# A gate product between up and down, both halves of down with seven-product units, and token sums from transposed rows

## The chip, the cores and the metric

The kernel runs on one core of a Trainium2 chip. The metric is the device time of one execution in microseconds (us), less is better; the time before is the median of three runs. The core has five engines that work side by side: TensorE (PE) for matmuls, VectorE (DVE), ScalarE (ACT), GpSimd (POOL), and SyncE (SP), which here only starts transfers from main memory (HBM). PE writes its results to eight banks of an accumulator memory (PSUM, 128 x 512 float32 each); everything else lies in the on-chip buffer (SBUF).

## The reference

One decoder layer on 256 tokens with 2048 channels in float32: a feed-forward network (FFN1), a mixing sub-layer with two kinds of attention, and a second network of the same shape (FFN2), each followed by a LayerNorm.

```python
def swiglu(x, w_gate, w_up, w_down):
    return (jax.nn.silu(x @ w_gate) * (x @ w_up)) @ w_down

x = layer_norm(DEEPNORM_ALPHA * x + FFN_RES_WEIGHT * swiglu(x, ffn1_w_gate[l], ffn1_w_up[l], ffn1_w_down[l]),
               ln1_g[l], ln1_b[l])
...
mix = jnp.concatenate([o_mla, o_nsa], axis=-1) @ w_out[l]
x = layer_norm(DEEPNORM_ALPHA * x + mix, ln2_g[l], ln2_b[l])
x = layer_norm(DEEPNORM_ALPHA * x + FFN_RES_WEIGHT * swiglu(x, ffn2_w_gate[l], ffn2_w_up[l], ffn2_w_down[l]),
               ln3_g[l], ln3_b[l])
```

The inner width of the networks is 5632. The change is in the two networks; the attention in between only gets its small tiles from a buffer pool that is cut in another way.

## The kernel before

**Products in three matmuls.** Every float32 operand is split into a rounded high part and a remainder (`split`, lines 80 to 82: ACT casts, DVE subtracts). `mm3` (lines 84 to 88) adds three matmuls for one product of a 128-row tile: high x high (line 86), high x low of the weight (87), low x high (88). So every weight that comes from HBM (`raw`) is cast by ACT into `whi` and gets its remainder `wlo` from DVE before PE can use it. There are five `raw`, three `sum`, six `whi` and six `wlo` buffers of 128 x 1024.

**The networks.** The 5632 inner columns are 11 blocks of 512, numbered 0 to 10, in groups 0 to 3, 4 to 7 and 8 to 10. For each group `ffn` (line 361) makes gate and up two blocks at a time, multiplies them, transposes the product (`hs`, rows are tokens) block by block into `hT`, and then adds the group's share of down to the result `y`. Block 10 of gate and up is made as one pair (`_gu`). The stages in order are: gate 0, 1; up 0, 1; gate 2, 3; up 2, 3; down of the first group (first half of the 2048 output columns, then the second); the same for the second group; gate 8, 9; up 8, 9; the combined product; down of the third group.

**Seven-product units.** `gemm2` (line 218) makes two column blocks for both token tiles at once. It walks over pairs of 128-row k tiles, of which there are eight in a product of gate and up or in the first two groups of down. A plain pair takes eight products, 24 matmuls. A pair listed in `seven` takes seven products (a two-by-two scheme of the Strassen kind), 21 matmuls: DVE first forms sums of the four weight tiles (lines 250 to 252), and the other side needs sums of the four tiles of the moving operand (`sums`, lines 298 to 305, with the pieces `m` made by `parts`). Behind the last such pair four partial results are merged (line 270 on ACT, lines 271 to 274 on DVE), and at the end four more additions join them with the plain part (line 282). Gate has three such pairs (`GATE7`), up four (`UP7`), the combined product four, and down four in the second half of the first two groups (`DOWN7`); the first half of down is plain (`gemm`, line 173).

**Order.** PE and SP run in the order in which the code is written. A clock of ticks (`tick`, `steps`) lets small tasks, such as the transposes, step in between pairs; `held` stops them while all eight PSUM banks are taken. ACT, DVE and POOL get their order from a scheduler, and each then works strictly in it.

**Where the sums of down come from.** When up of a block is multiplied (line 413), `up` starts two kinds of tasks. `go` (line 382) transposes four 128 x 128 tiles of a product on PE and splits them from PSUM. `go2` (line 392) does so for each pair that is to be done with seven products: DVE has formed the four sums from rows of `hs` before, PE transposes the four sums, and ACT and DVE split them from PSUM.

**Other names.** `wk` gives one of nine work tiles `w` of 128 x 512; `am` one of sixteen tiles `m` of the same size for pieces and for small operands of the attention. In FFN2 the list `late` holds four calls of `ln_res` (lines 523 to 531), each with two transfers on POOL's queue (lines 526, 527) and four DVE operations on `y` (530, 531); two calls stand behind each of the first two up products (lines 440 to 442).

## Time and profile before

| | us |
|---|---|
| median of three runs | 1785.65 |
| lowest, highest | 1784.14, 1786.55 |
| the profiled execution | 1784.83 |
| span in its trace | 1783.1 |

The profile is one execution. Its page gives the busy time of each engine, shares of the span, and groups of instructions by source line. The trace behind it is asked for a timeline (every instruction with its start and length), for windows (busy time of every engine in a stretch), and for waits (who waited for whom, inferred from semaphores). Matmuls overlap in the timeline: each starts before the one ahead has ended, so their spacing is read from their starts. Stages are found by counting matmuls of lines 86 to 88 from the start of each network.

FFN1 takes the first 714 us, with gate 4, 5 at 266.3, up 4, 5 at 307.8, gate 6, 7 at 348.6 and up 6, 7 at 391.4 us; the first half of down of the first group begins at 179.2 us. FFN2 begins at 1061.7 us, and its gate 2, 3 at 1151.6 us.

### The profile page before, as it was taken

Reading aid. Unit: us, or ns where it says so; the run is one execution under the profiler, and the core shown is the slowest. Engines: PE = TensorE matmul, PEld = TensorE weight load, DVE = VectorE, ACT = ScalarE, POOL = GpSimd, SP = SyncE. Lnnn points to the kernel's source line nnn. Section 1 sums busy time; section 2 is a strip of 40 time slices with the busy share of each in tenths; the row PEclk is TensorE's granted clock in tenths of the full one; section 3 lists DMA queues with packets and bytes.
Section 4 is the critical chain, followed back from the end, with each engine's and each line's share of the span. In section 5 each row is a group of like instructions: output and inputs, shape, how many; then the busy total and the mean of one; then the engine's idle time right before and its main releaser. Section 6 shows DMA issues by size and latency. Waiting matters only on the chain. (4 is left out here: it accounts for less than half of the span.)

```text
span 1783.1 us, 22369 instructions
## 1 busy us (share of the span) xinstructions
PE 1761.0 (99%) x8132; PEld 1445.5 (81%) x8132; DVE 1499.9 (84%) x1965; ACT 965.1 (54%) x1261; POOL 17.5 (1%) x40
## 2 busy tenths in 40 slices
PE   8999999999999999999999999999999999999997
PEld 6888888888888888887788777878888888888886
DVE  7899789999699986776567687899799998799976
ACT  6556455565456554654455555555456565456541
POOL 0000000000000000000000000000000000000000
PEclk9999999999999999999999999999999999999999
DMA  9666555557456675546743444657555656556673
GB/s 320 228 205 210 176 198 197 189 192 253 146 194 210 199 249 179 183 168 209 266 173 109 138 155 142 198 194 252 163 203 202 202 200 215 172 194 210 205 246 106
DMA packets 119423, 350.01 MB, mean 196 GB/s; under 512 B 11136, under 2 KB 15504, under 8 KB 119312
## 3 DMA queue, kind: packets, MB, share of 16 engines
q1 hardware_dynamic: 118000, 344.37, 57.1%
q0 software_dynamic: 1312, 4.21, 0.9%
q8 instruction: 64, 1.05, 0.2%
q14 instruction: 47, 0.39, 0.1%
HBM read 346.44 MB, written 2.10 MB: 195 GB/s over the span
## 5 line engine op out<-in xcount | busy, mean ns | idle before, releaser
L86 PE MATMUL bank<-whi,thi 128*128 128x512 f32 (+1 forms) x2038 | 804.0, 394 | 2.2 <-ACT thi L81 1.7
L87 PE MATMUL bank<-wlo,thi 128*128 128x512 f32 (+1 forms) x2038 | 792.3, 389 | 1.9 <-DVE wlo L82 1.9
L88 PE MATMUL bank<-whi,tlo 128*128 128x512 f32 (+1 forms) x2038 | 792.5, 389 | 0.1
L81 ACT CAST whi<-raw 128x1024 fp32r<-128x1024 f32 (+2 forms) x534 | 513.0, 977 | 412.4 <-PE bank L88 316.5
L82 DVE TENSOR_TENSOR wlo<-raw,whi 128x1024 fp32r<-128x1024 f32 (+2 forms) x534 | 594.9, 1130 | 104.4 <-ACT whi L81 104.1
L86 PEld LDWEIGHTS bank<-whi,thi 128*128 128x128 f32 x2038 | 383.0, 188 | 83.8 <-issue 4.5
L88 PEld LDWEIGHTS bank<-whi,tlo 128*128 128x128 f32 x2038 | 382.7, 188 | 81.3 <-DVE tlo L82 1.4
L87 PEld LDWEIGHTS bank<-wlo,thi 128*128 128x128 f32 x2038 | 383.1, 188 | 78.5 <-DVE wlo L82 3.7
L81 ACT CAST whi<-sum 128x1024 fp32r<-128x1024 f32 x262 | 271.7, 1048 | 279.9 <-PE bank L88 162.7
L82 DVE TENSOR_TENSOR wlo<-sum,whi 128x1024 fp32r<-128x1024 f32 x262 | 313.8, 1219 | 75.9 <-ACT whi L81 75.4
L87 PE MATMUL bank<-wlo,m 128*128 128x512 f32 x352 | 137.4, 390 | 0.2 <-DVE wlo L82 0.2
L88 PE MATMUL bank<-whi,m 128*128 128x512 f32 x352 | 137.0, 389 | 0.0
L86 PE MATMUL bank<-whi,m 128*128 128x512 f32 x352 | 137.0, 389 | 0.0
L250 DVE TENSOR_TENSOR sum<-raw 128x1024 f32<-128x1024 f32 x88 | 107.6, 1223 | 28.9 <-DMA raw<-in_ffn_w_gate 16.1
L87 PEld LDWEIGHTS bank<-wlo,m 128*128 128x128 f32 x352 | 66.1, 188 | 15.2 <-DVE wlo L82 1.6
L86 PEld LDWEIGHTS bank<-whi,m 128*128 128x128 f32 x352 | 66.1, 188 | 13.7
L88 PEld LDWEIGHTS bank<-whi,m 128*128 128x128 f32 x352 | 66.1, 188 | 13.7
L282 DVE TENSOR_TENSOR w<-bank,w 128x512 f32<-128x512 f32 x96 | 63.1, 686 | 0.0
L252 DVE TENSOR_TENSOR sum<-sum,raw 128x512 f32<-128x512 f32 x88 | 60.7, 690 | 0.7
L251 DVE TENSOR_TENSOR sum<-sum,raw 128x512 f32<-128x512 f32 x88 | 60.5, 688 | 0.3
L82 DVE TENSOR_TENSOR tlo<-bank,thi 128x512 fp32r<-128x512 f32 (+1 forms) x56 | 36.0, 649 | 4.0 <-ACT thi L81 3.6
L672 ACT ACTIVATE w<-w,mx 128x256 f32<-128x256 f32 (+1 forms) x48 | 21.4, 446 | 31.3 <-DVE mx L668 31.3
(187 smaller groups left out, 871.3 us busy)
## 6 DMA issues: line engine op xcount, KB each, us to landing
raw<-in_ffn_w_up SPq DMA_DIRECT2D x160, 512.0 KB, 4.7
raw<-in_ffn_w_gate SPq DMA_DIRECT2D x148, 512.0 KB, 4.8
raw<-in_ffn_w_down SPq DMA_DIRECT2D x134, 512.0 KB, 4.5
sum<-in_ffn_w_down SPq DMA_DIRECT2D x42, 512.0 KB, 6.4
raw<-in_ffn_gu SPq DMA_DIRECT2D x32, 512.0 KB, 4.8
raw<-in_w_in SPq DMA_DIRECT2D x30, 512.0 KB, 4.5
raw<-in_w_out SPq DMA_DIRECT2D x20, 512.0 KB, 3.2
sum<-in_w_in SPq DMA_DIRECT2D x18, 512.0 KB, 5.7
```

Source lines behind the costliest of these rows:

```text
L81: A.copy(hi, src)
L82: V.tensor_tensor(lo, src, f(hi), op=OP.subtract)
L86: PE.matmul(ps, xh, wh, start=first, stop=False)
L87: PE.matmul(ps, xh, wl, start=False, stop=False)
L88: PE.matmul(ps, xl, wh, start=False, stop=last)
L250: V.tensor_tensor(t13, a_, b_[:, 1:2, :].broadcast_to([P, 2, NCH]), op=OP.add)
L251: V.tensor_tensor(t24[:, 0], t13[:, 0], a_[:, 1], op=OP.add)
L252: V.tensor_tensor(t24[:, 1], t24[:, 0], b_[:, 0], op=OP.add)
L282: V.tensor_tensor(r, B[b], r, op=OP.add)
L672: A.activation(s[:, h, :], s[:, h, :], AF.Exp, bias=mx[:, h:h + 1], accum_out=sm[:, h:h + 1])
```

## The change

The stages of a network are written as one list: gate 0, up 0, gate 2, up 2, gate 4, down of the first group, up 4, gate 6, up 6, gate 8, down of the second group, up 8, the combined product, down of the third group (each number stands for two blocks). So a gate product lies between an up product and the down that reads it, and the transposes of that up product are done in its last pairs.

Both halves of down of the first two groups get four seven-product units; the combined product has three instead of four. The pairs of a product are taken in a given order (`GATE`, `UP`, `LATE`, `DOWN`), of which those in the lists with a 7 are seven-product units.

The sums for down are formed from the transposed rows: for blocks 0, 1 (and 4, 5) `trans` copies the transposed tiles from PSUM into a work tile, and DVE forms the sums of that. `go2` and its transposes are gone.

The tiles `m` are twice as wide, eight in place of sixteen, and are handed out as pairs (`am2`). The four calls in `late` stand in the second gate product of blocks 0, 1, which is plain.

```diff
@@ -34,10 +34,13 @@
 O_CKV, O_KR, O_Q, O_KC, O_KS, O_KW, O_G = 512, 768, 832, 1856, 2368, 2880, 3392
 KT = 2
 HEAD, SPARE = 8, 2
-NM = 16
+NM = 8
 NW = 9
-GATE7, UP7 = (2, 4, 5), (1, 2, 4, 5)
-DOWN7 = (((), (1, 2, 4, 5)), ((), (1, 2, 4, 5)), ((), ()))
+
+GATE, GATE7 = (0, 1, 2, 3, 4, 5, 6, 7), (2, 4, 5)
+UP, UP7 = (0, 1, 3, 2, 4, 6, 5, 7), (1, 2, 4, 5)
+LATE = (0, 3, 1, 6, 2, 4, 5, 7)
+DOWN, DOWN7 = (4, 0, 1, 5, 2, 3, 6, 7), (0, 1, 2, 3)
...
     def am(dt=F32):
-        return att.tile([P, 4, P], dt, name="m", bufs=NM)
+        return att.tile([P, 8, P], dt, name="m", bufs=NM)
+
+    def am2(dt=F32):
+
+        m = am(dt)
+        return m[:, 0:4, :], m[:, 4:8, :]
...
-    def gemm2(x, xs, seven, w, cp, kps, finish, each=None):
+    def gemm2(x, xs, kps, seven, w, cp, finish, each=None):
...
-        s_first, s_last = min(seven), max(seven)
+        s_at = [n for n, i in enumerate(kps) if i in seven]
...
-        for i, ops in todo:
+        for at, (i, ops) in enumerate(todo):
+            if at > s_at[-1]:
+                held[0] = False
...
-            if i == s_last:
+            if at == s_at[-1]:
...
-            held[0] = s_first - 1 <= i <= s_last
+            held[0] = s_at[0] - 1 <= at <= s_at[-1]
             tick(1)
             if each:
-                each(i)
...
     def parts(s):
-        hl = am(F32R), am(F32R)
+        hl = am2(F32R)
         split(*hl, s)
...
-        kall = list(range(KD // KT))
-        for gi, grp in enumerate(groups):
-            hT, hS, hs = {}, {}, {}
-            base = 2 * grp[0]
-            seven = [{base + i for i in DOWN7[gi][j]} for j in range(2)]
-
-            def up(c, t, h):
-
-                hs[c, t] = h
-
-                ready = now[0] + DFF
-
-                def go(c=c, t=t):
+        hT, hS, hs, sg = {}, {}, {}, {}
+
+        def trans(cs, ready, sums_too):
+
+            for c in cs:
+                v = []
+                for t in range(NT):
                     while held[0] or now[0] < ready:
                         yield 1
                     pt = new_bank().rearrange("p (a b) -> p a b", a=4)
                     for j in range(4):
                         PE.transpose(pt[:, j, :], hs[c, t][:, j * P:(j + 1) * P], ident)
                     hT[c, t] = new_T()
-                    split(hT[c, t][0], hT[c, t][1], pt)
+                    src = pt
+                    if sums_too:
+                        src = wk([P, 4, P])
+                        A.copy(src, pt)
+                        v.append(src)
+                    A.copy(hT[c, t][0], pt)
+                    V.tensor_tensor(hT[c, t][1], src, f(hT[c, t][0]), op=OP.subtract)
+                    if t and sums_too:
+                        for i in range(KT):
+                            hS[2 * c + i] = parts(sums([u[:, KT * i + j] for u in v for j in range(KT)]))
                     yield 1
-                def go2(i, s):
-                    while held[0] or now[0] < ready:
-                        yield 1
-                    pt = new_bank().rearrange("p (a b) -> p a b", a=4)
-                    for j in range(4):
-                        PE.transpose(pt[:, j, :], s[:, j, :], ident)
-                    hS[i] = parts(pt)
-                    yield 1
-
-                spawn(go(), "T")
-                if t:
-                    for i in (2 * c, 2 * c + 1):
-                        if i in seven[0] | seven[1]:
-                            spawn(go2(i, sums([hs[c, u][:, (2 * (i % 2) + j) * P:(2 * (i % 2) + j + 1) * P]
-                                               for u in range(NT) for j in range(2)])), "T")
-                steps()
-
-            for c0 in grp[::2]:
-                sg = {}
-
-                def gate(t, j, r):
+        def gate(c0):
+            def fin(t, j, r):
+                A.activation(r, r, AF.Silu)
+                sg[c0 + j, t] = r
+
+            if c0:
+                gemm2(x, xs, GATE, GATE7, name + "_w_gate", c0 // 2, fin)
+                return
+            def rest(i):
+                if i % 2 and late:
+                    late.pop(0)()
+
+            for c in range(2):
+                def first(t, ps, c=c):
+                    sg[c, t] = wk([P, NCH])
+                    A.activation(sg[c, t], ps, AF.Silu)
+
+                gemm(x, wg, c, list(range(KD)), first, head=0 if c or begin else HEAD, spare=SPARE,
+                     first=1 if c == 0 and begin else KT, each=begin if c == 0 else rest)
+
+        def up(c0):
+            def fin(t, j, r):
+                hs[c0 + j, t] = sg[c0 + j, t]
+                V.tensor_tensor(hs[c0 + j, t], r, sg[c0 + j, t], op=OP.mult)
+
+            gemm2(x, xs, LATE if c0 in (4, 8) else UP, UP7, name + "_w_up", c0 // 2, fin, each=after if c0 == 0 else None)
+            spawn(trans((c0, c0 + 1), now[0] + DFF, c0 in (0, 4)), "T")
+
+        def last():
+
+            def fin(t, j, r):
+                if j == 0:
                     A.activation(r, r, AF.Silu)
-                    sg[t, j] = r
-
-                def mult(t, j, r):
-                    h = sg[t, j]
-                    V.tensor_tensor(h, r, h, op=OP.mult)
-                    up(c0 + j, t, h)
-
-                def both(t, j, r):
-                    if j == 0:
-                        gate(t, 0, r)
-                    else:
-                        sg[t, 1] = sg[t, 0]
-                        h = sg[t, 0]
-                        V.tensor_tensor(h, r, h, op=OP.mult)
-                        up(c0, t, h)
-
-                if c0 == grp[-1]:
-
-                    gemm2(x, xs, UP7, name + "_gu", 0, kall, both)
-                    continue
-                if c0 == 0:
-                    for c in range(2):
-                        def first(t, ps, c=c):
-                            sg[t, c] = wk([P, NCH])
-                            A.activation(sg[t, c], ps, AF.Silu)
-
-                        gemm(x, wg, c, list(range(KD)), first, head=0 if c or begin else HEAD, spare=SPARE,
-                             first=1 if c == 0 and begin else KT, each=begin if c == 0 else None)
+                    hs[10, t] = r
                 else:
-                    gemm2(x, xs, GATE7, name + "_w_gate", c0 // 2, kall, gate)
-                gemm2(x, xs, UP7, name + "_w_up", c0 // 2, kall, mult, each=after if c0 == 0 else None)
-                for _ in range(2):
-                    if late:
-                        late.pop(0)()
+                    V.tensor_tensor(hs[10, t], r, hs[10, t], op=OP.mult)
+
+            gemm2(x, xs, GATE, GATE7, name + "_gu", 0, fin)
+            spawn(trans((10,), now[0] + DFF, False), "T")
+
+        def down(gi):
+            grp = groups[gi]
             ks = list(range(grp[0] * 4, (grp[-1] + 1) * 4))
             xh = lambda k, t: sl(hT[k // 4, t], k % 4)
-            def down(t, n, ps):
+            def fin(t, n, ps):
                 yc = y[t][:, n * NCH:(n + 1) * NCH]
                 if gi == 0:
                     V.scalar_tensor_tensor(yc, yc, 2 * ALPHA, ps, op0=OP.mult, op1=OP.add)
@@ -453,12 +452,20 @@
                     done(t, n)
             for cp in range(2):
-                if seven[cp]:
-                    gemm2(xh, hS, seven[cp], name + "_w_down", cp, list(range(base, 2 * grp[-1] + 2)),
-                          lambda t, j, r: down(t, 2 * cp + j, r))
+                if gi < 2:
+                    base = 2 * grp[0]
+                    gemm2(xh, hS, [base + i for i in DOWN], [base + i for i in DOWN7], name + "_w_down", cp,
+                          lambda t, j, r: fin(t, 2 * cp + j, r))
                     continue
                 for n in (2 * cp, 2 * cp + 1):
-                    gemm(xh, wd, n, ks, lambda t, ps: down(t, n, ps), tail=6 if gi == 2 and n == 3 else 0)
+                    gemm(xh, wd, n, ks, lambda t, ps: fin(t, n, ps), tail=6 if n == 3 else 0)
+
+
+        for step, n in ((gate, 0), (up, 0), (gate, 2), (up, 2), (gate, 4), (down, 0), (up, 4), (gate, 6), (up, 6), (gate, 8),
+                        (down, 1), (up, 8)):
+            step(n)
+        last()
+        down(2)
...
-    kcT, vcT = flat(am(), 2), flat(am(), 2)
...
```

On DVE, at the boundary from gate 6, 7 to up 6, 7 in FFN1, these rows stand between the first weights of up's first seven-product unit and its weight sums (`wlo<-sum`); `tlo` are remainders of transposed tiles, `w<-bank,w` the additions at the end of gate. Before:

```order
L250 TENSOR_TENSOR sum_3542<-raw_3538,raw_3539 128x1024
L82 TENSOR_TENSOR tlo_3407<-bank_3401,thi_3406 128x512
L282 TENSOR_TENSOR w_3323<-bank_3081,w_3323 128x512
L282 TENSOR_TENSOR w_3324<-bank_3089,w_3324 128x512
L282 TENSOR_TENSOR w_3325<-bank_3085,w_3325 128x512
L82 TENSOR_TENSOR tlo_3428<-bank_3422,thi_3427 128x512
L282 TENSOR_TENSOR w_3326<-bank_3093,w_3326 128x512
L82 TENSOR_TENSOR wlo_3506<-sum_3492,whi_3505 128x1024
```

Now, the last twelve rows ahead of the weight sums of that unit (`w` of 128x128 are token sums, `m` their pieces):

```order
L394 TENSOR_TENSOR tlo_3483<-w_3484,thi_3482 128x512
L313 TENSOR_TENSOR w_3488<-w_3488,w_3461 128x128
L312 TENSOR_TENSOR w_3496<-w_3484 128x128
L315 TENSOR_TENSOR w_3488<-w_3488,w_3461 128x128
L313 TENSOR_TENSOR w_3496<-w_3496,w_3461 128x128
L314 TENSOR_TENSOR w_3496<-w_3461,w_3484 128x128
L315 TENSOR_TENSOR w_3496<-w_3496,w_3461 128x128
L292 TENSOR_TENSOR w_3349<-bank_3109,w_3349 128x512
L292 TENSOR_TENSOR w_3350<-bank_3117,w_3350 128x512
L90 TENSOR_TENSOR m_3493<-w_3488,m_3493 128x512
L90 TENSOR_TENSOR m_3501<-w_3496,m_3501 128x512
L90 TENSOR_TENSOR wlo_3566<-raw_3553,whi_3565 128x512
```

The token sums of four pairs and their pieces have moved to this place, in front of the unit's remaining weights.

On PE, in the first group of FFN2, the transposes of blocks 2, 3 stood in the plain first half of down. Before:

```order
L87 MATMUL bank_10951<-wlo_11000,thi_10867 128x512
L88 MATMUL bank_10951<-whi_10999,tlo_10868 128x512
L382 MATMUL bank_11015<-ident_87,w_10429 128x128 x4
L382 MATMUL bank_11024<-ident_87,w_10430 128x128 x4
L86 MATMUL bank_10950<-whi_11035,thi_10511 128x512
```

Now they stand in the gate product ahead, the last of them between its last matmul and the first of down (`bank_11382`):

```order
L95 MATMUL bank_11015<-wlo_11317,thi_9604 128x512
L96 MATMUL bank_11015<-whi_11316,tlo_9605 128x512
L386 MATMUL bank_11353<-ident_87,w_10476 128x128 x4
L94 MATMUL bank_11382<-whi_11374,thi_11283 128x512
L95 MATMUL bank_11382<-wlo_11375,thi_11283 128x512
```

The transposes of rows have moved from down into the gate product, and those of sums (line 392 before) have no counterpart.

## Rows read from the trace of the kernel before

**Rows 1.** The page's first part: busy us (share of the span), instructions of each engine.

```profile
PE 1761.0 (99%) x8132; PEld 1445.5 (81%) x8132; DVE 1499.9 (84%) x1965; ACT 965.1 (54%) x1261; POOL 17.5 (1%) x40
```

**Rows 2.** PE's timeline: start us, length us, engine, line, operation, operands.

```profile
299.63 0.39 PE L86 MATMUL bank<-whi,thi 128*128 128x512 f32 x1
...
300.31 0.39 PE L86 MATMUL bank<-whi,thi 128*128 128x512 f32 x1
```

**Rows 3.** Stages as windows: span; busy per engine; granted clock, DMA share, GB/s.

```profile
core 0: us, PE busy (x) PEld busy (x) DVE busy (x) ACT busy (x) POOL busy (x), PEclk, DMA share, GB/s
179.20:225.50 46.30, 46.30 (x217) 38.48 (x216) 33.57 (x45) 19.31 (x22) 0.00 (x0) 1.00 0.53 177
266.30:307.80 41.50, 41.50 (x185) 34.35 (x184) 39.96 (x48) 22.51 (x25) 0.00 (x0) 1.00 0.60 204
307.80:348.60 40.80, 40.80 (x182) 33.78 (x181) 37.69 (x41) 25.05 (x28) 0.00 (x0) 1.00 0.62 206
348.60:391.40 42.80, 42.80 (x196) 35.44 (x195) 41.66 (x56) 22.53 (x26) 0.00 (x0) 1.00 0.58 194
391.40:433.80 42.40, 42.40 (x196) 35.07 (x195) 40.88 (x48) 27.83 (x33) 0.00 (x0) 1.00 0.66 223
...
1151.60:1196.80 45.20, 43.88 (x197) 35.16 (x195) 43.87 (x60) 21.97 (x25) 2.19 (x4) 1.00 0.60 195
```

**Rows 4.** Waits of PE, whole run: who for whom, us, times, longest us.

```profile
PE bank L87 <- DVE wlo L82: 2.1, 3, 1.1
```

**Rows 5.** Waits of all engines, whole run, the longest of ACT.

```profile
ACT whi L81 <- PE bank L88: 479.2, 352, 8.5
```

**Rows 6.** The middle stretch of FFN1 and of FFN2 as windows.

```profile
53.10:645.20 592.10, 592.10 (x2664) 490.31 (x2663) 537.41 (x627) 330.07 (x368) 0.00 (x0) 1.00 0.60 201
1110.80:1705.50 594.70, 593.38 (x2666) 490.00 (x2664) 547.27 (x643) 329.05 (x368) 4.35 (x8) 1.00 0.61 203
```

**Rows 7.** DVE's timeline, weights of the first unit of up, columns 4 and 5.

```profile
297.80 1.22 DVE L82 TENSOR_TENSOR wlo<-raw,whi 128x1024 fp32r<-128x1024 f32 x1
```

**Rows 8.** PE's timeline, the first matmul on those weights.

```profile
308.02 0.39 PE L87 MATMUL bank<-wlo,thi 128*128 128x512 f32 x1
```

**Rows 9.** DVE's timeline in FFN2's gate of columns 2, 3: the residual.

```profile
1161.58 1.30 DVE L530 TENSOR_TENSOR y<-y,w 128x512 f32<-128x512 f32 x2
```

**Rows 10.** PE's timeline behind it; in brackets the idle time and its releaser.

```profile
1169.23 0.50 PE L87 MATMUL bank<-wlo,thi 128*128 128x512 f32 x1 [1.09 <-DVE wlo L82]
```

**Rows 11.** DVE's timeline, operations of 512, 1024 and 128 columns in a row.

```profile
301.26 0.68 DVE L274 TENSOR_TENSOR w<-bank,w 128x512 f32<-128x512 f32 x1
301.86 1.21 DVE L250 TENSOR_TENSOR sum<-raw 128x1024 f32<-128x1024 f32 x1
302.99 1.22 DVE L82 TENSOR_TENSOR wlo<-raw,whi 128x1024 fp32r<-128x1024 f32 x1
...
352.47 0.29 DVE L302 TENSOR_TENSOR w<-w 128x128 f32<-128x128 f32 x1
352.67 0.29 DVE L304 TENSOR_TENSOR w<-w 128x128 f32<-128x128 f32 x1
```

**Rows 12.** DVE's timeline, FFN1, boundary from gate to up of columns 6, 7.

```profile
394.97 2.36 DVE L82 TENSOR_TENSOR wlo<-sum,whi 128x1024 fp32r<-128x1024 f32 x2
```

**Rows 13.** PE's timeline, first use of those weights.

```profile
399.71 0.39 PE L87 MATMUL bank<-wlo,m 128*128 128x512 f32 x1
```

**Rows 14.** Two windows of FFN2, with granted clock (PEclk).

```profile
1160.00:1170.00 10.00, 8.71 (x37) 6.59 (x36) 9.67 (x13) 3.68 (x4) 0.54 (x1) 1.00 0.45 149
1200.00:1240.00 40.00, 40.00 (x181) 32.66 (x180) 39.67 (x45) 25.27 (x30) 0.00 (x0) 1.00 0.73 243
```

**Rows 15.** PE's timeline, at the start of the run.

```profile
6.95 0.63 PE L86 MATMUL bank<-m,thi 128*128 128x512 f32 x1
7.38 0.63 PE L87 MATMUL bank<-m,thi 128*128 128x512 f32 x1
```

More of the change, by code (lines that the diff above doesn't have):

```diff
@@ L984, in out_last @@
             steps()
[L986 removed]
+    qrT += am2()
     gemm(lambda k, t: sl(cq[t], k), uq, 2, list(range(4)), fin_qr, nxt=(uq, 0, 0))
```

14 lines of the change are left out of this document (8 added, 6 removed).

## The prediction

> **What bounds the kernel now.** I read the page's engine rows first: TensorE (PE) is busy for 99% of the span and VectorE (DVE) for 84% [rows 1]. "Busy" overlaps itself on PE. A product matmul is 0.39 us long, but in the timeline the third one after it starts 0.68 us later, so each costs 0.2267 us [rows 2]; removing one from the path gives that and not 0.39. The stages agree: the up product of columns 4 and 5 is 180 matmuls in 40.80 us, 0.2267 each [rows 3]. PE hardly waits: for low halves of weights, three times and 2.1 us in the whole run [rows 4]. So the time is the number of matmuls and transposes, as long as the operands are there.
>
> Whether they are there depends on DVE, which writes the low halves of all weights, the weight sums of the seven-product units and the sums at the ends. It is the next engine: in the gate and up stages shown it is busy 92 to 97% of the time, in the plain first half of down 73% [rows 3]. Over the middle stretch, from up of columns 0, 1 to the combined gate/up product, it does 537.41 us of work in 592.10 us in FFN1 (the first feed-forward network) and 547.27 in 594.70 us in FFN2 [rows 6]. What saves PE is a lead: weights for the first unit of the up product at 307.8 are written from 297.80 to 299.02 us [rows 7], and PE uses them at 308.02 us [rows 8], 9.0 us later. Buffers bound the lead: ScalarE (ACT) waits 479.2 us in all for PE to give weight buffers back [rows 5].
>
> **Part 1, fewer products.** A plain pair of k tiles is 24 matmuls, a seven-product unit 21. The first half of down gets four such units in two groups of two FFNs: 16 units, 48 matmuls fewer. The combined gate/up product goes from four to three units in each FFN: 6 more. Net 42 x 0.2267 = **-9.5 us**, all on the path.
>
> **Part 2, token sums from transposed rows.** The sums were made from rows and then transposed (line 392, 64 transposes in 16 groups of four); now they are made from rows that are transposed anyhow. What a group costs on PE is read between stages: gate of columns 6, 7 has three groups and takes 42.80 us, gate of 4, 5 has none and takes 41.50 (0.43 each); up of 6, 7 has three, 42.40 against 40.80 (0.53 each); the plain half of down has six, 46.30 against 192 x 0.2267 = 43.5 (0.47 each) [rows 3]. With 0.45: 16 x 0.45 = **-7.2 us** (bounds -6.9 and -8.5). DVE's count for the sums stays; ACT gets 20 copies more, and at 54% [rows 1] it has room.
>
> **Part 3, the residual of the second LayerNorm.** These 16 DVE operations, with their transfers on GpSimd's queue, now stand beside the second plain gate product of FFN2, where weights ask least of DVE. Before, they stood after the ups: six of them (three rows of two, the first at 1161.58 us [rows 9]) stand between the weights of a seven-product unit, and PE then idles for the low half of a weight, 1.09 us in one wait [rows 10]. That gate stage takes 45.20 us in FFN2; its equal without the residual, gate of 6, 7 in FFN1, takes 42.80 [rows 3]. Removed: **-2.4 us**. In the new place a late transfer stops DVE and the weights queued behind, but not PE while a lead like the 9 us covers it. Bounds -2.4 and 0.
>
> **Part 4, what DVE gets.** From start to start, 1024 columns take 1.13 us, 512 take 0.60 and 128 take 0.20 [rows 11]. A seven-product unit costs DVE 4 x 1.13 + 3 x 0.60 = 6.3 us against 4.76 us of PE; a plain pair 2.26 against 5.44. Each FFN gets 8 - 1 = 7 more units (7 x 4.06 = 28.4) and 16 merge operations more (9.6): 38 us. Less the moved residual (16 x 0.60 = 9.6 in FFN2), the middle stretch then asks for 575.4 us of DVE in FFN1 and 575.7 in FFN2. PE's side of it is 592.10 - 4.8 - 3.6 = 583.7 us. **DVE is needed for 98.6% of that time.** On this point the forecast stands or falls.
>
> [...]
>
> Stage by stage (units, merge 2.4, adds of the stage before 2.4, its products or additions to y 2.4, low halves of transposes 2.4, sums with their pieces 5.6): gate with sums (columns 2, 3 and 6, 7) asks for 45.5 of 43.3 us; gate of 4, 5 and 8, 9 for 39.9 of 43.3; up behind a gate and the first half of down for 39.1 of 40.8; the second half of down and up behind down for 41.5 of 40.8. The worst run, second half, up, gate with sums, is short by 0.7 + 0.7 + 2.2 = 3.6 us, less than the 9 us of lead. So no stage's total starves PE; a burst can.
>
> **The burst.** At the boundary from gate with sums to up, DVE works in order. Before, the weight sums of the first seven-product unit are written from 394.97 us (two in 2.36 us, the first done at about 396.2) [rows 12] and used at 399.71 [rows 13]: a lead of 3.5 us, behind six operations of 0.60 us. Now 28 operations stand there (12 of 0.60, 16 of 0.20: 10.4 us), 6.8 us more. The bounds are 0 (DVE comes there earlier, since buffers held it) and 6.8 - 3.5 = 3.3 us. Followed from the last transpose at the boundary: ACT has a weight cast, a piece and a copy ahead of the sums (1.05 + 0.6 + 0.6 = 2.3 us, sized as DVE's steps), DVE then 8 small and 5 large operations (4.6) and two weights (1.7): 8.6, with the hand-overs 8.9 us. PE wants them after 24 + 10 matmuls, 7.7 us. I take 1.2 us at each of four such boundaries: **+4.8 us** (0 to 13). All later weights stand behind, but the delay is paid once. For the four second halves and the four ups behind down I take **+1 us** (0 to 8 x 0.7 = 5.6, if no lead were left).
>
> Work tiles: there are nine; four hold gate values over both halves of down and four the merge, and at the four boundaries the sums' copies wait for a free one, within the 1.2 us. Pieces now come in pairs, eight buffers for sixteen; attention uses them too. No row shows a pair that is freed late; the nearest is PE's 2.1 us [rows 4]: I take 0, bounds -2.1 and +2.1. Transfers: the same bytes; with five buffers for raw weights, as in the gate and up stages now, which run at a DMA share of 0.58 to 0.66 [rows 3].
>
> **Sum.** 1784.83 us (the profiled execution; span 1783.1) - 9.5 - 7.2 - 2.4 + 4.8 + 1.0 = 1771.5; the median of the three runs is 0.8 us above the profiled one, so **1772 us**.
>
> **Rivals.**
> A. Nothing waits: 1784.8 - 19.1 + 0.8 = 1766.5. For it: from 1200 to 1240 us DVE is busy 39.67 of 40.00 us and PE is never idle [rows 14]. Against: the lead at the burst is only 3.5 us.
> B. Every shortage is paid in full, because no lead is left from the stage before: per FFN 2 x 2.2 + 4 x 0.7 = 7.2, in both 14.4: 1781. For it: in FFN2's first group DVE was behind, and PE lost 2.4 us. Against: the 9 us.
> C. Slower: DVE becomes the bound and cannot be kept busy. Place: the middle stretches. With DVE busy for a share s, each takes 575.5 / s us. They stand at 592.10 and 594.70, so the change loses below s = 1151 / 1186.8 = 97.0%. At 96% the time is 1784.8 + 12.2 + 0.8 = 1798. For it: from 1160 to 1170 us, where PE did wait, DVE was busy 9.67 of 10.00 us, just 96.7% [rows 14], since it waits for ACT's casts in order. Against: 99% from 1200 to 1240.
> [...]
> That the change does not do what it says is out for PE: the program has 42 matmuls and 64 transposes fewer.
>
> **How the numbers follow.** Forecast (1767 to 1779) 0.50; A 0.15; B 0.18; C 0.13; D 0.02; attention's pairs, either way, 0.02. Measurements of this kernel tell 0.2% (3.6 us) from no change, so faster means under 1782.1: 0.50 + 0.15 + two thirds of B = 0.77. The rest of B and the pairs are the same, 0.08; C and D slower, 0.15. The range goes from A with part 2's far bound, 1765, through B to the near edge of C, 1789.
>
> **What would show it.** Right: no transposes of sums; middle stretches of 585 to 588 us with DVE at 98%; new waits of PE for low halves of weights at the four boundaries, about 1 us each; FFN2's first gate stage with sums as short as FFN1's. A: no such waits. B: waits also in the second halves of down and the ups behind them. C: DVE at 95 to 97% in the middle stretches, PE waiting all along. Wrong altogether: waits of PE for banks, or a longer attention.

## The result: 1772.4 us, 0.7% less

The changed kernel takes 1772.37 us (median of four runs, 1770.68 to 1774.08), the kernel before 1785.86 us beside it: a ratio of 0.9926, 95% interval 0.9909 to 0.9943. The forecast was 1772.0 us, with a range from 1765 to 1789. The profiled execution took 1772.05 us, 12.8 us less than that of before.

The page's engine row, which answers [rows 1]: PE has 106 instructions fewer (42 products, 64 transposes), and DVE has gone from 84% to 89% of a shorter span.

```profile
PE 1746.8 (99%) x8026; PEld 1431.5 (81%) x8026; DVE 1567.2 (89%) x2067; ACT 987.5 (56%) x1309; POOL 17.4 (1%) x40
```

Stages of the changed kernel as windows (length; busy us per engine; granted clock, DMA share, GB/s): gate of columns 2, 3 and up of 2, 3 in FFN1, a second half of down, gate of 2, 3 in FFN2, and the two middle stretches, which answer [rows 3, 6].

```profile
94.70:138.00 43.30, 43.30 (x201) 35.87 (x200) 42.00 (x56) 24.57 (x30) 0.00 (x0) 1.00 0.59 195
138.00:180.30 42.30, 41.52 (x183) 33.65 (x182) 42.22 (x56) 26.75 (x34) 0.00 (x0) 1.00 0.59 190
264.50:305.30 40.80, 40.80 (x182) 33.73 (x181) 40.74 (x47) 23.02 (x25) 0.00 (x0) 1.00 0.59 198
1147.90:1191.20 43.30, 43.30 (x201) 35.85 (x199) 42.42 (x57) 24.82 (x30) 0.00 (x0) 1.00 0.59 199
53.90:641.40 587.50, 585.79 (x2617) 482.96 (x2615) 573.27 (x680) 341.19 (x393) 0.00 (x0) 1.00 0.62 205
1107.10:1693.60 586.50, 585.36 (x2617) 483.11 (x2616) 575.71 (x685) 341.21 (x393) 0.00 (x0) 1.00 0.61 204
```

The middle stretches went from 592.1 and 594.7 us to 587.5 and 586.5. DVE is busy for 97.6% and 98.2% of them, and in up of columns 2, 3 and the second half of down it doesn't pause at all. Only up of 2, 3 is longer than its 180 products (40.8 us): there PE waits. ACT's and PE's waits over the whole run (who for whom: us, times, longest us) answer [rows 4, 5]:

```profile
ACT whi L89 <- PE bank L96: 255.1, 197, 8.5
ACT whi L89 <- DVE sum L262: 138.2, 77, 6.1
ACT whi L89 <- DVE sum L260: 112.1, 47, 5.6
...
PE bank L95 <- DVE wlo L90: 3.9, 9, 0.8
```

Before, ACT's longest waits for sums on DVE were:

```profile
ACT whi L81 <- DVE sum L252: 56.9, 32, 3.6
ACT whi L81 <- DVE sum L250: 24.5, 21, 5.9
```

PE's waits for low halves grew from 2.1 to 3.9 us; start to start they cost more, as shown below. ACT's waits tell what became of the lead: before, it waited 479.2 us for PE to give weight buffers back, since the weights ran ahead of their use, and 81.4 us for sums on DVE. Now it waits 255.1 us for PE and 250.3 us for sums on DVE. Much of the lead has been spent.

How it is spent shows at the boundary from gate to up of columns 2, 3 in FFN1. DVE's timeline (start us, length us), then PE's:

```profile
141.86 0.28 DVE L312 TENSOR_TENSOR w<-w 128x128 f32<-128x128 f32 x1
...
143.07 0.68 DVE L90 TENSOR_TENSOR m<-w,m 128x512 fp32r<-128x512 f32 x1
...
144.47 0.68 DVE L90 TENSOR_TENSOR wlo<-raw,whi 128x512 fp32r<-128x512 f32 x1
145.07 0.68 DVE L90 TENSOR_TENSOR m<-w,m 128x512 fp32r<-128x512 f32 x1
145.68 2.35 DVE L90 TENSOR_TENSOR wlo<-sum,whi 128x1024 fp32r<-128x1024 f32 x2
```

```profile
145.78 0.40 PE L94 MATMUL bank<-whi,m 128*128 128x512 f32 x1
146.95 0.50 PE L95 MATMUL bank<-wlo,m 128*128 128x512 f32 x1 [0.78 <-DVE wlo L90]
```

Sums (128 columns), their pieces (`m`) and the adds stand in DVE's order ahead of the weight sums of the first seven-product unit. At the boundary shown for before (columns 6, 7), those came 3.5 us early [rows 12, 13]; now PE starts on them the moment they are there, 1.17 us after its last product, 0.94 more than a product takes.

In what follows a stage runs from the start of its first product to the start of the next stage's first, and its floor is its products times 0.2267 us. What a stage takes above floor and transposes (0.45 us for each group) is its loss. Not all of it is waiting: where the last group of a gate product stands right at its end, the first products behind it come 0.13 us late, and this is booked in the up stage.

### The profile page after: what moved, and what is told of

It is laid out like the page before. It is cut to its first block, busy times and chain, and to the rows that moved or that the text cites. A ratio compares the mean times of both kernels' runs of the same rounds, so it can differ in the third digit from the quotient of the medians.

```text
span 1770.3 us, 22326 instructions
## 1 busy us (share of the span) xinstructions
PE 1746.8 (99%) x8026; PEld 1431.5 (81%) x8026; DVE 1567.2 (89%) x2067; ACT 987.5 (56%) x1309; POOL 17.4 (1%) x40
## 4 chain that ended last, share of the span: by engine, by line
PE 83%; DVE 12%; DMA 2%; issue 2%; ACT 1%; SPq 0%; POOL 0%; DVEq 0%; ACTq 0%; POOLq 0%
PE bank L94 26%; PE bank L95 26%; PE bank L96 26%; DVE wlo L90 5%; DVE sum L260 1%; DMA raw<-in_ffn_w_up 1%; DVE w L292 1%; ACT whi L89 1%; DMA raw<-in_ffn_w_down 1%; DVE sum L262 1%; PE bank L386 1%; PE bank L950 1%; DVE sum L261 1%; PE bank L940 1%; DVE tlo L394 1%
## 5 line engine op out<-in xcount | busy, mean ns | idle before, releaser
L94 PE MATMUL bank<-whi,thi 128*128 128x512 f32 (+1 forms) x1968 | 776.3, 394 | 2.0 <-ACT thi L89 1.7
L95 PE MATMUL bank<-wlo,thi 128*128 128x512 f32 (+1 forms) x1968 | 765.7, 389 | 1.9 <-DVE wlo L90 1.9
L96 PE MATMUL bank<-whi,tlo 128*128 128x512 f32 (+1 forms) x1968 | 765.4, 389 | 0.1
L90 DVE TENSOR_TENSOR wlo<-raw,whi 128x1024 fp32r<-128x1024 f32 (+2 forms) x558 | 614.2, 1115 | 74.8 <-ACT whi L89 74.5
L89 ACT CAST whi<-sum 128x1024 fp32r<-128x1024 f32 (+1 forms) x266 | 277.9, 1050 | 370.7 <-DVE sum L262 138.2
L90 DVE TENSOR_TENSOR wlo<-sum,whi 128x1024 fp32r<-128x1024 f32 (+1 forms) x266 | 318.6, 1214 | 48.7 <-ACT whi L89 47.1
L95 PE MATMUL bank<-wlo,m 128*128 128x512 f32 x408 | 159.6, 391 | 2.0 <-DVE wlo L90 2.0
L94 PE MATMUL bank<-whi,m 128*128 128x512 f32 x408 | 158.8, 389 | 0.0
L96 PE MATMUL bank<-whi,m 128*128 128x512 f32 x408 | 158.8, 389 | 0.0
L94 PEld LDWEIGHTS bank<-whi,m 128*128 128x128 f32 x408 | 76.6, 188 | 16.0
L96 PEld LDWEIGHTS bank<-whi,m 128*128 128x128 f32 x408 | 76.6, 188 | 15.5
L386 PEld LDWEIGHTS bank<-ident,w 128*128 128x128 f32 x176 | 21.9, 140 | 5.8
```

The lines of the kernel that those rows point to most:

```text
L89: A.copy(hi, src)
L90: V.tensor_tensor(lo, src, f(hi), op=OP.subtract)
L94: PE.matmul(ps, xh, wh, start=first, stop=False)
L95: PE.matmul(ps, xh, wl, start=False, stop=False)
L96: PE.matmul(ps, xl, wh, start=False, stop=last)
L386: PE.transpose(pt[:, j, :], hs[c, t][:, j * P:(j + 1) * P], ident)
```

## The experiments

Each kernel was timed against the kernel before on the same chip, whose median there was 1785.4 to 1786.4 us. Edits are to the changed kernel, unless said otherwise.

**The changed kernel again.**

> The changed kernel once more, unaltered, on the same chip as the three that follow. Theory: 1772.4 us (1770.7 to 1774.1), as in its first comparison; PE's waits for low halves of weights at the four gate-to-up boundaries within 0.3 us of what they were.

Measured 1771.65 us (1771.30 to 1774.16), 0.9922 (0.9910 to 0.9935). The four boundaries lost 0.7, 1.2, 1.2 and 1.5 us (1.5, 1.4, 1.1 and 1.2 in the first profile): 4.6 against 5.2 in all, though not each within 0.3. The four second halves of down lost 2.2 against 1.0: 1.4 in the first of FFN1, where the first profile shows nothing. So the sum, 6.2 and 6.8 us, is much the same in the two profiles, and the place of a single wait is not.

**Without the sums.**

```diff
-   src = wk([P, 4, P])
-   A.copy(src, pt)
-   v.append(src)
    ...
-   hS[2 * c + i] = parts(sums(...))
+   hS[2 * c + t] = hT[c, t]
```

> The work that makes the token sums of down is left out (the copies of transposed rows, the sums, their two pieces); the seven-product units of down multiply a pair of transposed tiles in their place, so PE's program is unchanged and the output is not the reference's. Theory (the burst at four boundaries costs 5.2 us, and its lag some 1 us in the second halves of down): 1766 to 1767.5 us, with no wait over 0.4 us at the four boundaries. Rival (those waits come from ScalarE's order or from weight buffers, not from the sums): 1771 to 1773, the waits stay.

Measured 1764.87 us (1764.47 to 1765.51), 0.9882 (0.9868 to 0.9895): 7.5 us less than the changed kernel and 1.1 below the range expected. Windows of up of columns 2, 3 and of FFN1's middle stretch:

```profile
137.80:178.80 41.00, 41.00 (x183) 33.93 (x182) 37.85 (x42) 25.68 (x29) 0.00 (x0) 1.00 0.58 192
...
53.80:637.90 584.10, 584.10 (x2616) 483.53 (x2616) 563.43 (x641) 337.16 (x377) 0.00 (x0) 1.00 0.61 205
```

All waits in the middle stretches are gone, and they take 584.1 us, within 0.4 us of the floor the prediction set (583.7). So the waits came from the sums' work. ScalarE had less to do as well (377 operations for 393 in FFN1's stretch: copies and casts of pieces), so this run by itself does not tell which of the two engines PE waited for. The changed kernel's trace does: at the boundary shown above ScalarE had cast both weight sums by 142.08 us, and DVE, which did not pause, came to them at 145.68. Nor does the run say whether the amount of DVE's work counts or its place.

**Fewer units, and the order.** First the first halves of down in plain pairs; then that, with down put back right behind up.

```diff
-   if gi < 2:
+   if gi < 2 and cp:
```

> The first halves of both downs go back to plain pairs (four seven-product units fewer in each of four places), all else as changed: 48 products more on PE. Theory (PE's count sets the time, DVE has just enough slack): +48 x 0.2267 = +10.9 us against the changed kernel, less at most the 1 us that PE now waits in the second halves of down: 1782 to 1783.3 us. Rival O (the gain comes from the gate product put between up and down, not from the count): no change, 1772. Rival C (DVE sets the pace of the middle stretches): DVE gets 4 x (4 x 4.06 + 4.8) = 84 us less to do, so no loss and perhaps a gain: 1772 or less.

```diff
-   ... (gate, 4), (down, 0), (up, 4), (gate, 6), (up, 6), (gate, 8), (down, 1), (up, 8)
+   ... (down, 0), (gate, 4), (up, 4), (gate, 6), (up, 6), (down, 1), (gate, 8), (up, 8)
```

> As the kernel with plain first halves of down (1780.0 us), and down now again right behind up of columns 2, 3 and 6, 7, the gate product behind it: only the place of one gate product in each group changes. Theory (the place brings nothing by itself, it only makes the units in the first half possible): 1780 us (1778 to 1782). Rival O (the gate product between them is itself a gain, as cover for transposes): 1784 or more. Rival (the burst's lag runs into the gate product behind it, and a plain half would give it cover at once): 1776 to 1778.

Measured 1780.03 us (1779.06 to 1782.21; 0.9966, 0.9954 to 0.9978) and 1780.00 us (1777.53 to 1780.64; 0.9966, 0.9952 to 0.9979). The first half of down in the first kernel, then in the second, as windows:

```profile
222.40:266.10 43.70, 43.70 (x194) 36.17 (x194) 26.75 (x28) 18.67 (x21) 0.00 (x0) 1.00 0.50 179
```

```profile
178.20:223.60 45.40, 45.40 (x210) 37.67 (x209) 32.74 (x37) 18.37 (x20) 0.00 (x0) 1.00 0.57 198
```

From the first product to the next stage's first, twelve products more take 43.65 - 40.93 = 2.72 us in each of four stages, 10.9 us: the price of a product holds. The median rose by 7.7 us, less than the 9.6 to 10.9 expected; the intervals of the two ratios are wide enough for either, and the profiled execution of the first kernel, its slowest, is 10.2 us behind that of the changed one. The order alone shows no worth in the medians: the four groups of transposes just move, from the gate product into the half of down (+1.7 us there). These runs also weigh amount against place a first time: DVE has some 38 us less to do in each middle stretch (535 to 538 us, 90 to 91%), the second halves of down lose nothing any more, yet the four boundaries still lose 5.5 us in the first kernel and 3.4 in the second.

**The same relief at two places.** Two seven-product units, not three, in the gate products that end in the burst (columns 2, 3 and 6, 7), or in the other two, with `(4, 8)` in place of `(2, 6)`.

```diff
-   gemm2(x, xs, GATE, GATE7, name + "_w_gate", c0 // 2, fin)
+   gemm2(x, xs, GATE, GATE7[:2] if c0 in (2, 6) else GATE7, ...)
```

> The gate products of columns 2, 3 and 6, 7 (those that end in the burst of sums) get two seven-product units, not three: 12 products more on PE, +2.7 us, and 4 x 4.06 = 16.2 us less on DVE, right ahead of the burst. The changed kernel's waits for DVE are 5.2 us at the boundaries and 1 to 2 us in the second halves of down. Burst theory and total theory both: those waits go to 1 to 3 us in all: 1769 to 1771 us. Rival (the waits at the boundary don't depend on DVE's lead): 1774.5.

> The same relief in the other gate products (columns 4, 5 and 8, 9): 12 products more, 16.2 us less on DVE, but not ahead of the burst. Total theory: as the run with the relief ahead of the burst, 1769 to 1771 us. Burst theory: the 4.6 to 5.2 us at the boundaries stay and only the waits in the second halves of down go: 1772.5 to 1773.5 us.

Measured 1767.68 us (1766.85 to 1768.10), 0.9895 (0.9879 to 0.9911), ahead of the burst, 1.3 us below the range expected, and 1772.52 us (1769.81 to 1773.47), 0.9920 (0.9907 to 0.9933), behind it. Windows of up of columns 2, 3 and of FFN1's middle stretch, ahead:

```profile
138.20:179.00 40.80, 40.80 (x181) 33.78 (x181) 40.74 (x47) 26.50 (x31) 0.00 (x0) 1.00 0.61 204
53.30:638.80 585.50, 585.50 (x2620) 484.66 (x2620) 566.64 (x671) 342.01 (x388) 0.00 (x0) 1.00 0.61 205
```

and behind:

```profile
137.10:178.60 41.50, 41.23 (x183) 33.74 (x182) 41.42 (x54) 26.58 (x34) 0.00 (x0) 1.00 0.57 183
...
53.00:639.70 586.70, 586.16 (x2623) 484.46 (x2621) 566.85 (x670) 339.42 (x389) 0.00 (x0) 1.00 0.60 204
```

PE has the same number of products in both, and DVE the same work (566.64 and 566.85 us). Ahead of the burst every wait in the middle stretches is gone; behind it the second halves of down are free, and the boundaries still lose 0.7, 0.7, 0.7 and 0.8 us, 2.9 in all in place of 5.2. So the amount of DVE's work counts, since the relief behind the burst took away half of the loss, and at the same amount the place counts: from start to start the middle stretches are 1.2 and 1.3 us shorter with the relief ahead. The medians are 4.8 us apart, more than these 2.5. The rest is not shown to come from the place: of the five executions with the relief behind the burst, the two with a mean granted clock of 0.998 took 1769.8 and 1770.2 us, and the three with 0.997 took 1772.5 to 1773.5. The version with the relief ahead of the burst is faster than both kernels of this case: 12 products more, and 4 to 5 us less than the changed kernel.

**A later first unit.** Up of columns 2, 3 and 6, 7 in the order of up of 4, 5.

```diff
-   gemm2(x, xs, LATE if c0 in (4, 8) else UP, UP7, ...)
+   gemm2(x, xs, LATE if c0 else UP, UP7, ...)
```

> The up products of columns 2, 3 and 6, 7 take their pairs in the order that up of 4, 5 and 8, 9 already has (first seven-product unit third, not second); nothing else, the same work on every engine. Burst theory (the sums stand 5.2 us in front of the first unit): one more plain pair gives DVE 3.2 us more before the first unit is due, so the boundaries lose 0 to 2 us instead of 5.2: 1767 to 1770 us. Total theory (DVE is asked for 575.5 us in each middle stretch and can be kept busy for 98% of it, so the stretches take 587 us in any order): 1772.4 us, the waits move to later units.

Measured 1774.79 us (1772.40 to 1779.66), 0.9940 (0.9926 to 0.9954): no gain. The boundaries did become almost free (1.0 us in all), but gate of columns 8, 9, which had lost nothing, now takes 45.7 and 45.6 us for 43.3. DVE's timeline just before, then PE's:

```profile
429.12 1.29 DVE L292 TENSOR_TENSOR w<-bank,w 128x512 f32<-128x512 f32 x2
...
432.71 1.29 DVE L423 TENSOR_TENSOR w<-w 128x512 f32<-128x512 f32 x2
433.91 3.50 DVE L90 TENSOR_TENSOR wlo<-raw,whi 128x1024 fp32r<-128x1024 f32 x3
```

```profile
435.19 0.50 PE L95 MATMUL bank<-wlo,thi 128*128 128x512 f32 x1 [2.10 <-DVE wlo L90]
```

The eight operations that finish up (adds and products, 4.8 us) stand ahead of the next weights: a second burst, at every end of an up product with units. Here the last three units stand in a row with one plain pair behind them, and up hands over with no lead; in the changed kernel's up of 2, 3 and 6, 7 a plain pair lies between them. That this is the reason is not shown: up of 4, 5 has the late order in the changed kernel too, and gate of 6, 7 behind it loses nothing. Both theories had their share right here: the first burst was relieved, and the time came out as if the total were fixed.

**The residual put back** behind up of columns 0, 1 and of 2, 3.

```diff
-   if i % 2 and late:
-       late.pop(0)()
    ...
    step(n)
+   for _ in range(2):
+       if late and step is up:
+           late.pop(0)()
```

> The 16 operations of FFN2's residual go back behind the first two up products, all else as changed. Theory: FFN2's gate of columns 2, 3 gets its 2.4 us back, since six of them stand between weights there, and the rest is covered: 1774.8 us (up to 1777 as DVE is tighter now). Rival C (no slack on DVE in the middle stretch at all): +16 x 0.60 = +9.6: 1782. Rival (the move was worth nothing): 1772.

Measured 1783.59 us (1781.21 to 1790.55), 0.9990 (0.9981 to 0.9999): 11.2 us more than the changed kernel, nearly the whole gain, and nearest to what rival C gave. My figure of 2.4 us was far off here. FFN2's gate 2, 3, up 2, 3, gate 4, 5 and middle stretch as windows, and PE's longest wait:

```profile
1145.50:1190.90 45.40, 44.01 (x199) 35.56 (x198) 44.04 (x62) 23.22 (x30) 1.60 (x3) 1.00 0.58 200
1190.90:1237.20 46.30, 42.89 (x183) 34.96 (x182) 45.37 (x59) 29.02 (x35) 0.54 (x1) 0.96 0.59 186
1237.20:1283.40 46.20, 44.07 (x201) 35.61 (x200) 45.30 (x56) 22.98 (x28) 1.61 (x3) 1.00 0.61 206
1104.70:1702.70 598.00, 588.86 (x2617) 483.81 (x2615) 583.62 (x697) 340.76 (x393) 3.75 (x7) 1.00 0.60 203
```

```profile
1200.32 0.50 PE L95 MATMUL bank<-wlo,thi 128*128 128x512 f32 x1 [3.41 <-DVE wlo L90]
```

Eight of the operations (4.8 us) stand ahead of the burst, eight behind it. The stretch takes 598.0 us in place of 586.5, and not only the gate stage but the three stages in a row lose (2.2, 4.4 and 2.9 us against the changed kernel). The same 9.6 us of DVE work cost 2.4 us in the kernel before, where DVE had slack, nothing that the stages show in the changed kernel, where most of it stands beside a plain gate product, and 11.5 us here. The row of up 2, 3 also shows a granted clock of 0.96; the last section comes back to it.

**More work in a stage without waits.** The low halves of the first pair's weights in gate of 4, 5 and 8, 9 are written twice.

```diff
+   if again and at == 0:
+       V.tensor_tensor(lw[:, :n], v[:, :n], f(hi[:, :n]), op=OP.subtract)
```

> In gate of columns 4, 5 and 8, 9, where PE never waits in the changed kernel, the low halves of the first pair's weights are written twice: 2 x 1.13 us more of DVE in four stages, 9.0 us in all, the result the same. Lead theory (DVE idles 1.2 us in such a stage and 0.5 us in the half of down behind it, and the lead there is 2 to 9 us): part of it is absorbed, 1774 to 1777 us. Total theory (DVE has no time left anywhere in the middle stretch, being kept busy for at most 98%): +9.2 us wherever it is put, 1781 us, with the new waits in the second half of down or up behind it. Rival (only the burst at the boundaries counts): 1772.

Measured 1788.20 us (1782.61 to 1790.19), 1.0010 (1.0001 to 1.0019): 16 us more, beyond all three expectations. The edit did more than I meant. DVE's order is the scheduler's, and it set the second write of the second weight (L270) behind the eight operations that end up; then PE:

```profile
176.22 1.22 DVE L90 TENSOR_TENSOR wlo<-raw,whi 128x1024 fp32r<-128x1024 f32 x1
...
182.14 1.29 DVE L425 TENSOR_TENSOR w<-w 128x512 f32<-128x512 f32 x2
183.34 1.23 DVE L270 TENSOR_TENSOR wlo<-raw,whi 128x1024 fp32r<-128x1024 f32 x1
```

```profile
184.62 0.50 PE L95 MATMUL bank<-wlo,thi 128*128 128x512 f32 x1 [2.61 <-DVE wlo L270]
```

The weight had been finished once at 177.4 us; its second copy came at 184.6. PE's two products around the wait start 3.0 us apart, 2.8 more than a product takes. Four such waits are 11 us, and behind three of them the granted clock fell: behind the one shown it is 0.74 and then 0.83 over 4 us each, around the second of FFN1 it stays at 1.00 (434 to 450 us), and its mean is 0.99 both from 1120 to 1400 and from 1400 to 1700 us. So this run doesn't measure slack, as it was meant to. It shows again what stands behind the end of a product: one operation of 1.1 us there cost 2.8 us, and 4.5 with the fall of the clock.

**Sums from rows.** The sums made from rows and transposed, as before the change, one unit's at a time.

```diff
+   v.append(sums([hs[c, u][...] for u in range(NT) for j in range(KT)]))
    ...
+   PE.transpose(pt[:, j, :], s[:, j, :], ident)
```

> The token sums are made from rows again and transposed on PE (16 groups of four transposes more), their pieces taken a little later, one unit's at a time; all else as changed. Theory: +16 x 0.45 = +7.2 us, less what of the 5.2 us of waits at the four gate-to-up boundaries goes because the sums now stand earlier on DVE: 1774.4 to 1779.6 us; a gate stage with sums or the stage behind it gets longer by 0.45 us for each group in it. Rival (a transpose that reads rows already there is hidden between products): 1767 to 1772.

Measured 1792.52 us (1788.56 to 1796.39), 1.0039 (1.0025 to 1.0053), 13 us above the range expected. PE waits for the sums themselves (first fence: us, times, longest us), and the products behind are then 0.43 us apart (second: timeline, start us, length us):

```profile
PE bank L399 <- DVE w L312: 9.4, 4, 2.3
```

```profile
439.51 1.68 PE L399 MATMUL bank<-ident,w 128*128 128x128 f32 x4 [2.34 <-DVE w L312]
...
441.84 0.63 PE L96 MATMUL bank<-whi,tlo 128*128 128x512 f32 x1
442.27 0.63 PE L94 MATMUL bank<-whi,thi 128*128 128x512 f32 x1
```

Transposes that read a sum stand in PE's order and make all products behind them wait for DVE. That is 9.4 us of waits, some 4 us by which the waiting groups themselves took longer, and some 7 us by which the products behind them did at 0.43 us each, beside the price of 16 groups. I placed them too close behind their sums, so the run does not isolate the transposes; the stages above do that. In this profiled execution, the slowest of the five, the clock fell at all four waits: its mean is 0.99 in each of the stretches 100 to 300, 300 to 640, 1120 to 1400 and 1400 to 1700 us, and 0.991 in the whole run.

**Sums on GpSimd.**

```diff
-   hS[2 * c + i] = parts(sums([...]))
+   hS[2 * c + i] = parts(sums([...], G))
```

> The 128-column operations of the token sums (128 in all, 0.20 us each on DVE) are done by GpSimd; the copies, the pieces and the rest stay. DVE gets 12.8 us less per FFN and the burst is 3.2 us shorter at each boundary. Burst theory: the four boundaries lose 0 to 2 us: 1767 to 1770 us, with the low end only if GpSimd's operations slow none of DVE's. Rival (GpSimd is slower per operation, and DVE waits for its sums to write the pieces, with weights queued behind): 1772 to 1785, DVE waits for GpSimd at the boundaries.

(The count there is wrong: it is 64 operations in all, 6.4 us per FFN.) Measured 1781.07 us (1779.95 to 1783.96), 0.9976 (0.9966 to 0.9986), 9 us slower than the changed kernel: the rival was right. The timeline of GpSimd (POOL), ACT and DVE at the boundary:

```profile
142.85 1.48 DVE L90 TENSOR_TENSOR wlo<-sum,whi 128x1024 fp32r<-128x1024 f32 x1
...
143.21 1.44 POOL L312 TENSOR_TENSOR w<-w 128x128 f32<-128x128 f32 x1
...
144.61 0.45 POOL L315 TENSOR_TENSOR w<-w 128x128 f32<-128x128 f32 x1
...
145.10 0.62 ACT L89 CAST m<-w 128x512 fp32r<-128x512 f32 x1 [2.71 <-POOL w L315]
...
145.75 0.70 DVE L90 TENSOR_TENSOR m<-w,m 128x512 fp32r<-128x512 f32 x1 [1.42 <-ACT m L89]
```

An operation takes 0.45 us on GpSimd alone and up to 1.44 beside DVE, and DVE's operation of 1024 columns 1.48 in place of 1.22. ACT waits for the sums, DVE for ACT, and the weights stand behind: the four up stages take 44.1 to 45.6 us.

**A unit moved to the combined product.** The faster version, with a fourth unit in the combined gate/up product.

```diff
-   gemm2(x, xs, GATE, GATE7, name + "_gu", 0, fin)
+   gemm2(x, xs, UP, UP7, name + "_gu", 0, fin)
```

> As the kernel with two units in the gate products that end in the burst (1767.7 us), and the combined gate/up product gets its fourth seven-product unit back: 6 products fewer on PE, 4.06 us more of DVE in each FFN, put where the plain last part of down follows and DVE is busy for 75% of the time. Burst theory (DVE's work costs only where a unit stands close behind it): -6 x 0.2267 = -1.4 us, 1766.3 us (1765.5 to 1767.2), no new wait. Total theory (DVE at 98% of the stretch, so each microsecond asked for is paid): +1 to +6 us against 1767.7, with waits for low halves in the combined product or at the start of the last part of down.

Measured 1769.83 us (1769.12 to 1771.97), 0.9912 (0.9898 to 0.9926): 2.1 us more than the faster version, not 1.4 less; the intervals of the two ratios overlap, but all five executions lie above the range forecast. DVE and PE in FFN2, start of the combined product:

```profile
1647.75 1.27 DVE L292 TENSOR_TENSOR w<-bank,w 128x512 f32<-128x512 f32 x2
...
1651.35 1.28 DVE L423 TENSOR_TENSOR w<-w 128x512 f32<-128x512 f32 x2
1652.55 0.68 DVE L262 TENSOR_TENSOR sum<-sum,raw 128x512 f32<-128x512 f32 x1
```

```profile
1654.42 0.50 PE L95 MATMUL bank<-wlo,thi 128*128 128x512 f32 x1 [1.83 <-DVE wlo L90]
```

The fourth unit comes second in the stage, right behind the eight operations that end up of 8, 9. My expectation counted what follows the unit, not what stands ahead of it. (In the last part of down of the faster version DVE is busy for 63 to 67% of the time, not 75.) The last part of down in FFN2 lost 1.6 us more than in the faster version as well, 0.9 of it in one pause of PE that ended with ScalarE's cast of a transposed tile. In FFN1 the same order cost no such wait, and the stage lost 0.3 us; why the two differ stays open.

## Why the prediction was right

**Part 1, -9.5 us: right.** PE's counts fell as said, and the runs with plain first halves give 2.72 us for 12 products.

**Part 2, -7.2 us: right, a little too small.** The gate stages seem to give the 0.45 us that I took (43.28 us with four groups, floor 41.49). But the last of a gate's groups stands at its end and leaves 0.13 us to the up stage behind. With that a group costs 0.48 us there, and where a gate has room for all of it, in the run with two units ahead of the burst, it does too (44.09 us with four groups, floor 42.17). Without it the up stages of before come to the same: up of 6, 7 took 42.37 us with three groups, floor 40.81, and 0.13 of that belonged to the gate ahead. So the two prices that I read, 0.43 and 0.53 [rows 3], were one price cut at two places, and 16 groups are -7.7 us.

**Part 3, -2.4 us: right as a difference from before.** FFN2's gate of columns 2, 3 went from 45.17 to 43.29 us, with one group more in it: -2.3 us. What the prediction didn't say is that the rest of the gain hangs on it. Its sum for DVE already counted the 9.6 us as gone; with them back the stretch asks for more than PE needs (575.7 + 9.6 = 585.3 us against 583.7), and the run cost 11.2 us.

**Part 4: DVE's demand was right, and so was the burst.** Forecast 575.4 and 575.7 us of work, measured 573.27 and 575.71. The four boundaries lost 5.2 us, of which 4.7 are waits and the rest the four times 0.13 us of transposes (forecast 4.8), the second halves of down 1.0 and the ups behind them nothing (together forecast at 1.0). The runs without sums and with the relief at two places show that it is the burst in front of the first unit that PE pays for, and that how much it pays hangs on the lead that DVE brings there. Two steps stand on less than the numbers suggest. The 0.3 us for hand-overs in the chain of 8.9 us are on no row of before, so part of the closeness may be luck. And a DVE operation was priced from start to start; at its full length, 1.22 us for 1024 columns and 0.68 for 512 [rows 11], the added operations (14 of the first size, 37 of the second) would by my estimate ask for some 4 us more and leave 583.7 - 575.4 - 4 = 4.3 us of slack. The work measured (573.27 and 575.71 us) fits the price from start to start.

**The sum.** -9.5 - 7.7 - 2.3 + 4.7 + 1.0 = -13.8 us; the first gate product of FFN1 (48.67 for 47.91 us) and attention (348.4 for 347.4) add 1.7 and give -12.1, measured -12.8. The 1.7 looks like scatter: the changed kernel's second profile has 48.3 and 347.4. So the pieces in pairs cost attention nothing that both profiles show, as forecast. The 0.7 left over lies mostly in FFN2's up of 2, 3, which before took 0.3 us more than up of 6, 7, and in the last parts of down, which are 0.3 us shorter each beyond their groups. These and the 0.5 us too little in part 2 stand against the scatter, which nobody forecast; that they nearly cancel is luck, and the forecast hit the time closer than its terms.

**The rivals.** A (nothing waits, 1766.5) is what leaving the sums out gives, 1764.9, and what the faster version nearly reaches. B (every shortage is paid) would have cost 14.4 us; 5.7 were paid. In the gate products and the first halves of down DVE paused for 0.4 to 2.0 us each, so it had caught up there. C (DVE cannot be kept busy) has its place at 97.0%: the changed kernel kept DVE busy for 97.6 and 98.2%, only a little past it, and the residual put back (583.62 of 598.00 us, 97.6% again) shows how near the edge is. (The 0.33 us that DVE paused from 1160 to 1170 us of before ended with a transfer of `in_ln_b`, not with a cast of ACT.) D (the clock falls at PE's new waits) did not come: the granted clock is 1.00 in all middle stages, where PE's longest pause was 1.2 us. No row of before shows such a fall, so its chance, 0.02, was an estimate without a measurement behind it. In four of the experiments (sums from rows, residual put back, halves written twice, sums on GpSimd), where PE paused for longer, the clock did fall: behind 9 of 18 new pauses of 2.0 to 3.8 us, at a cost of 1.1 to 2.4 us each.

**What stays open.** Why the same program loses 1.4 us in a second half of down in one execution and nothing in another; and how much slack DVE has left in the stages without waits, since the run meant for it changed the order.

## What to carry to other kernels

When a change buys cheap work on the busiest engine with work on the next one, first work out what share of the time the second needs: at 98% the time still followed the first but for 6 us, and one step of 9.6 us put back cost 11.2. Then look for the places where many operations of the second engine end up in a row ahead of something that the first needs soon; here an equal relief took away all the waits when it stood ahead of such a place, and about half of them behind it. Moving the due work later only moved the wait to the next such place, so look at what stands ahead of an edit, not only at what follows.

## What the runs showed of the hardware

**The granted clock behind pauses of PE.** PE's timeline in the run with low halves written twice, behind the wait shown above, and eight microseconds of it as windows:

```profile
184.95 0.39 PE L96 MATMUL bank<-whi,tlo 128*128 128x512 f32 x1
...
185.88 0.57 PE L94 MATMUL bank<-whi,thi 128*128 128x512 f32 x1
186.24 0.63 PE L95 MATMUL bank<-wlo,thi 128*128 128x512 f32 x1
...
189.52 0.39 PE L94 MATMUL bank<-whi,thi 128*128 128x512 f32 x1
```

```profile
184.00:188.00 4.00, 3.38 (x11) 2.70 (x12) 4.00 (x5) 0.00 (x0) 0.00 (x0) 0.74 0.56 176
188.00:192.00 4.00, 4.00 (x16) 3.26 (x15) 4.00 (x5) 2.02 (x3) 0.00 (x0) 0.83 0.79 284
```

PE stood still for 3.0 us between two starts, went on with products 0.23 us apart for 1.3 us, and then they came 0.43 us apart for some 3 us, with a granted clock of 0.74 and 0.83 in the two windows: 1.6 us lost beyond the wait. In the run with the residual put back the granted clock is 0.60 from 1202 to 1206 us, behind the wait of 3.41 us. (The kernel before also starts its run with products 0.43 us apart [rows 15], but with a granted clock of 1.00 from 6.9 to 7.9 us, so the spacing alone does not tell the clock.) Counted over the 14 profiled executions, their first 15 us aside: pauses of 1.0 to 1.9 us were never followed by such a stretch of slow products; the pause of 2.13 us at the start of FFN2, which every execution has, in 5 of 14; other pauses of 2.0 to 2.5 us in 1 of 9; pauses of 2.7 to 3.8 us in 8 of 9, twice 0.3 us before PE went on. Each time the products behind took 1.1 to 2.4 us longer in all. What decides between the cases of 2.13 us was not found; it is one source of the scatter between executions: the first gate product of FFN2 took 50.7 us with such a stretch and 49.1 without.

**GpSimd beside DVE.** In the run with sums on GpSimd an operation of 128 columns took 0.45 us while DVE was idle and up to 1.44 beside it, and DVE's of 1024 columns took 1.48 for 1.22 us. Beside a DVE addition that reads one operand from PSUM, an operation of GpSimd at 141.92 us took 0.46 us. Why the lengths differ is not shown.
